# Mixer B's values through an SBUF copy, a gate tile between two head groups, and inverse square roots in eight operations

## The chip, the core and the metric

The kernel runs on one core of a Trainium2 chip. A core has five engines with queues of their own: PE (TensorE, matrix products; PEld is its loading of the stationary operand), ACT (ScalarE), DVE (VectorE), POOL (GpSimd) and SP (SyncE, which here issues most transfers). Products land in PSUM, eight banks of 128 x 512 float32; everything else works on SBUF. The metric is the device time of one execution in microseconds. Before the change it was 1541.07 us, the median of three runs (1538.99 to 1541.78).

## The reference

Two layers on an input of 512 tokens by 1024 channels. Each layer has a mixing half and a channel half, both with residual additions:

```python
h = rms_norm(x, norm_mix[l]);  z = h @ w_in[l]
qa, ka, va, qi, ki, wi, cq, ckv, kr, ga, gb = split_cols(z)
y_a = sparse_indexed_attention(...)          # mixer A: 8 heads, top 128 keys by an indexer
qb = (rms_norm(cq) @ b_w_uq[l])              # mixer B: 8 heads of 64 + 32 (rotated) columns
kv = (rms_norm(ckv) @ b_w_ukv[l])            # 64 key columns and 64 value columns per head
kb = concat(kv[..., :64], rope(kr));  vb = kv[..., 64:]
y_b = latent_attention(rms_norm(qb), rms_norm(kb), vb)
merged = sigmoid(ga + ...) * (y_a @ w_proj_a[l]) + sigmoid(gb + ...) * (y_b @ w_proj_b[l])
x = x + merged @ w_out[l]
u = causal_dwconv(rms_norm(x) @ w_up[l]);  x = x + (silu(u[..., d_ff:]) * u[..., :d_ff]) @ w_down[l]
```

The norm of a head's key takes the mean square over its 96 columns: 64 of its own and 32 rotated ones that all heads share. The norms' inverse square roots are what the change calls rsqrt.

## The kernel before, in words

**Products in two parts.** Float32 precision is had from PE's faster format by splitting every operand into a high part (a cast, ScalarE) and a low part (the operand minus its cast, VectorE) and adding three products: high by high, high by low, low by high. `split_into` (L299 to L306) is the helper for activations: the cast is L302, the subtraction L303; where a scale is applied they are L305 and L306. Weight tiles of up to 128 x 1024 are loaded by SP (L156) in the order of `dense_plan`, cast by ScalarE (L173), and their low part comes from VectorE (L185) or, for the kinds listed in `DL` (gb, ga, uv, ug, kv, uq), from a negated ScalarE copy (L201) onto which a DMA issued by POOL adds the tile (L202).

**PSUM.** Four rings of banks: D (2) for dense tiles, L (3) for scores and for mixer B's projections, T (2) for transposes and norm sums, Y (1) for attention outputs. A bank can be written again when every engine has read what was in it.

**Order.** The program is written as interleaved generators. `mix_dense` yields after every few matmuls; it produces the indexer's products, the latents, mixer B's two head groups (`attn_b(0)` and `attn_b(1)`), the eight gate tiles gb, mixer A's groups, and the gate tiles ga. While the attention heads of mixer B run (`mixer("yb", ...)`), a feeder calls `mix_dense` at a given rate per step, so that dense matmuls stand between those of the attention. `later(n, f)` puts a piece of work n steps further on. From this a scheduler makes the final order of every engine's queue; it may move an instruction ahead of others on its engine. The queues themselves run strictly in order. The indexer's top-k search (`top_k`, L1014 and L1021 on VectorE) is spread over the same steps.

**A head group of mixer B** (`attn_b`). For each of four blocks of 128 tokens, six matmuls (L834) write 256 key columns and 256 value columns of four heads into an L bank. Then:

```python
A.copy(k4[t][:, :, 0:64], p[:, 0:4])                            # L840
split_into(v[:, :, 0:64], v[:, :, 64:128], p[:, 4:8])           # L302 and, a step later, L303
squares(p[:, 0:4], ssk[:, t], 64)                               # L821, and L822 on VectorE
```

So two engines read the bank. The queries' four blocks follow: nine matmuls each (L871) into an L bank, a copy (L877) and squares (L821). `keys` (L848, L849) and `queries` (L896) make the mean squares, rsqrt gives the factors, and the keys (L858) and queries (L902) are scaled on VectorE; POOL rotates and completes them. `turn_b` transposes a head's queries and keys on PE (L1127) and splits them (tbh, tbl); `scores_b` computes scores in four blocks of 128 queries with 128, 256, 384 and 512 keys (L1142 to L1144, one L bank each), VectorE takes the maximum (L1145), and ScalarE the exponential with its sum (L357, an activation and a read of the accumulator). `softmax_end` normalises, `values` transposes the probabilities (L1052) and multiplies them with the values (L1059).

**rsqrt** (L331 to L346): a first guess by integer arithmetic (L334), then three Newton steps of three VectorE operations each (L343 to L345): ten operations on tiles of 128 x 4 or 128 x 16.

## Time and profile before

| what | value |
|---|---|
| median of the runs | 1541.07 us (1538.99 to 1541.78) |
| the profiled execution | 1542.47 us, of which the span is 1540.8 us |
| granted PE clock | 1.00 throughout |
| PE busy | 1528.9 us, 99% |
| VectorE / ScalarE / POOL busy | 1124.0 / 945.9 / 395.0 us |

The span goes from the first to the last instruction. In the rows below an instruction stands with its line, engine, operation, output and inputs; a wait row reads engine, tile and line, what it waited for, then microseconds in total, times, and the longest. PE's matmuls overlap, so a busy PE is not a PE at its peak, and a stop of PE is best measured from start to start.

### The profile page before, as it was taken

What the parts mean: (1) busy time and instruction counts of PE and PEld (TensorE: products, weight loads), DVE (VectorE), ACT (ScalarE), POOL (GpSimd) and SP (SyncE); (2) the same over time, 40 slices, a digit from 0 to 9 for tenths busy, and PEclk for the clock granted to TensorE, in tenths of its full rate; (3) what the DMA queues carried; (4) which work ended last, traced back from release to release, by engine and by line L of the source; (5) the groups of instructions that cost most, each with busy time, mean ns of one, the idle gap of its engine ahead of it and who ended that gap; (6) DMA issues with size and microseconds to landing.
All of it is one profiled execution on the core that took longest, in us unless ns stands there. A gap on an engine that the chain in (4) does not pass through costs nothing.

```text
span 1540.8 us, 23967 instructions
## 1 busy us (share of the span) xinstructions
PE 1528.9 (99%) x8666; PEld 1337.1 (87%) x8666; DVE 1124.0 (73%) x2303; ACT 945.9 (61%) x1553; POOL 395.0 (26%) x578
## 2 busy tenths in 40 slices
PE   9999999999999999999999999999999999999998
PEld 8887999888888898889998889998888888988898
DVE  7899988666476693547979999885574857845577
ACT  7756677773577536665557677686635765456642
POOL 2343012300012331125502520223001115311355
PEclk9999999999999999999999999999999999999999
DMA  7464124733478448873554641356435783588723
GB/s 245 104 160 122 46 92 110 186 120 119 127 189 190 103 117 219 191 178 96 151 165 112 166 99 56 103 135 173 131 99 144 177 190 95 152 197 195 176 77 109
DMA packets 73575, 216.29 MB, mean 140 GB/s; under 512 B 8432, under 2 KB 11504, under 8 KB 73456
## 3 DMA queue, kind: packets, MB, share of 16 engines
q1 hardware_dynamic: 54592, 149.08, 31.0%
q0 software_dynamic: 18432, 65.28, 22.6%
q8 instruction: 68, 1.11, 0.3%
q14 instruction: 51, 0.42, 0.1%
q10 hardware_dynamic: 432, 0.40, 0.1%
HBM read 141.06 MB, written 4.19 MB: 94 GB/s over the span
## 4 chain that ended last, share of the span: by engine, by line
PE 82%; DVE 12%; ACT 3%; issue 1%; POOL 0%; DMA 0%; DVEq 0%; ACTq 0%
PE D L516 35%; PE T L516 15%; PE D L539 6%; PE L L1424 5%; PE T L1424 4%; PE D L1424 3%; DVE sc L1021 2%; PE Y L1059 2%; DVE m L1014 2%; PE Y L1424 2%; PE T L1052 2%; PE L L516 2%; PE L L324 1%; PE L L323 1%; PE L L706 1%
## 5 line engine op out<-in xcount | busy, mean ns | idle before, releaser
L173 ACT CAST wh<-wr 128x1024 fp32r<-128x1024 f32 (+2 forms) x205 | 211.2, 1033 | 164.4 <-PE D L516 73.5
L202 POOL DMA_DIRECT2D wl<-wr x128 | 110.8, 877 | 633.0 <-ACT wl L201 604.4
L516 PE MATMUL D<-hxh,wh 128*128 128x512 f32 (+1 forms) x440 | 174.2, 396 | 0.0
L516 PE MATMUL D<-hxl,wh 128*128 128x512 f32 (+1 forms) x440 | 172.9, 393 | 0.0
L201 ACT ACTIVATE wl<-wr 128x1024 fp32r<-128x1024 f32 (+2 forms) x128 | 132.2, 1035 | 47.9 <-PE D L516 25.7
L191 ACT CAST wh<-wr 128x896 fp32r<-128x896 f32 x88 | 82.7, 941 | 103.8 <-POOL wr L215 69.6
L1093 POOL TENSOR_TENSOR P<-M,sel 128x128 f32<-128x128 f32 (+1 forms) x64 | 54.5, 907 | 272.9 <-DMA M<-in_bias_dram 239.3
L516 PE MATMUL D<-hxh,wl 128*128 128x512 f32 (+1 forms) x440 | 117.9, 393 | 0.0
L539 PE MATMUL D<-wh,hxh 128*128 128x256 f32 x384 | 113.8, 297 | 0.0
L196 DVE TENSOR_TENSOR wl<-wr,wh 128x896 fp32r<-128x896 f32 x88 | 103.8, 1181 | 8.2 <-ACT wh L191 3.1
L215 POOL TENSOR_TENSOR wr<-wr 128x256 f32<-128x256 f32 x88 | 93.8, 1068 | 60.8 <-DVE wr L214 48.3
L539 PE MATMUL D<-wl,hxh 128*128 128x256 f32 x384 | 109.3, 285 | 0.0
L539 PE MATMUL D<-wh,hxl 128*128 128x256 f32 x384 | 108.4, 283 | 0.0
L185 DVE TENSOR_TENSOR wl<-wr,wh 128x1024 fp32r<-128x1024 f32 x77 | 95.4, 1245 | 6.6 <-ACT wh L173 5.6
L516 PE MATMUL D<-hrl,wh 128*128 128x512 f32 x256 | 99.6, 389 | 0.0
L516 PE MATMUL D<-hrh,wh 128*128 128x512 f32 x256 | 99.6, 389 | 0.0
L516 PE MATMUL T<-hrh,wh 128*128 128x512 f32 x256 | 99.6, 389 | 0.0
L516 PE MATMUL T<-hrl,wh 128*128 128x512 f32 x256 | 99.6, 389 | 0.0
L516 PEld LDWEIGHTS D<-hxh,wh 128*128 128x128 f32 x440 | 82.9, 188 | 13.4 <-DVE gb L680 0.2
L516 PEld LDWEIGHTS D<-hxl,wh 128*128 128x128 f32 x440 | 82.9, 188 | 12.7
L516 PEld LDWEIGHTS D<-hxh,wl 128*128 128x128 f32 x440 | 80.2, 188 | 14.0
L1368 DVE SCALAR_TENSOR_TENSOR c<-T,vec,c 128x511 f32<-128x511 f32 x32 | 23.9, 748 | 89.1 <-ACT c L1365 89.1
(454 smaller groups left out, 4577.2 us busy)
## 6 DMA issues: line engine op xcount, KB each, us to landing
wr<-in_wd_dram SPq DMA_DIRECT2D x197, 512.0 KB, 3.7
wl<-wr POOLq DMA_DIRECT2D x120, 512.0 KB, 5.3
wr<-in_wd_dram SPq DMA_DIRECT2D x88, 256.0 KB, 2.6
x<-in_xT_dram SPq DMA_DIRECT2D x16, 256.0 KB, 4.8
M<-in_bias_dram SPq DMA_DIRECT2D x16, 256.0 KB, 4.0
wr<-in_wd_dram SPq DMA_DIRECT2D x7, 384.0 KB, 3.3
kah<-kah SPq DMA_DIRECT2D x16, 128.0 KB, 4.5
kal<-kal SPq DMA_DIRECT2D x16, 128.0 KB, 3.7
```

Source lines behind the costliest of these rows:

```text
L173: ins = self.nc.scalar.copy(h[:, :n], t[:, :n])
L185: eng.tensor_tensor(out=o[:, c], in0=t[:, c], in1=h[:, c].bitcast(F32), op=OP.subtract)
L191: self.nc.scalar.copy(h[:, :896], t[:, 128:1024])
L196: self.later(lag, lambda: self.nc.vector.tensor_tensor(out=o[:, :896], in0=t[:, 128:1024], in1=h[:, :896].bitcast(F32), op=OP.subtract))
L201: self.nc.scalar.activation(o, t, AF.Copy, scale=-1.0)
L202: self.nc.gpsimd.dma_start(o.bitcast(F32), t, accum_op=OP.add)
L215: g(2)(out=b[:, 6:8], in0=b[:, 0:3:2], in1=b[:, 3:6:2], op=OP.add)
L516: mm(p[:, t0:], lhsT=w, rhs=x[:, t0:], start=n == 0, stop=n == len(seq) - 1, skip_group_check=True)
L539: mm(pp[b][:, t, :], lhsT=x, rhs=w, start=n == 0 and half == 0 and t == 0, stop=n == 11 and half == 1, skip_group_check=True)
L1014: ins = V.max(out=m8[i], in_=st["sc"][i][:, :128 * (i + 1)])
L1093: G.tensor_tensor(out=P[:, P0[i]:P0[i] + w], in0=M[:, 512 - w:512], in1=sel[:, SEL0[i]:SEL0[i] + w], op=OP.add)
L1424: mm(p, lhsT=w, rhs=x, start=b0, stop=b1, skip_group_check=True)
```

## The change

Three edits, and one that follows from the third.

1. The value columns are copied out of PSUM by ScalarE into one half of an SBUF tile vr, which two token blocks share; the cast and the subtraction of the split read this copy.
2. GB_1 goes from 4 to 5: in the weight plan and in the program, the fifth gate tile (gb, 4) comes after `attn_b(0)` and before `attn_b(1)`, where before all of tiles 4 to 7 came after both.
3. rsqrt makes one Newton step and one step of third order: eight VectorE operations. It can write its result to a given tile, so the norm's copy into rstd (L467) goes.
4. The keys' mean square is one VectorE operation in place of two. The shared rotated part is divided by 96 and given its epsilon once per layer on POOL.

```diff
-NEWT = 1
+CUBE = 0.375 ** 0.5
-GB_1 = 4
+GB_1 = 5
-    def rsqrt(a, shape, quick=False):
+    def rsqrt(a, shape, out=None):
 
         y, t = small("y", shape), small("t", shape)
         V.tensor_scalar(y.bitcast(I32), a.bitcast(I32), -0.5, float(0x5F3759DF), op0=OP.mult, op1=OP.add)
...
-        for _ in range(3):
-            V.tensor_tensor(out=t, in0=y, in1=y, op=OP.mult)
-            V.scalar_tensor_tensor(t, t, -0.5, a, op0=OP.mult, op1=OP.mult)
-            V.scalar_tensor_tensor(y, t, 1.5, y, op0=OP.add, op1=OP.mult)
-        return y
+        V.tensor_tensor(out=t, in0=y, in1=y, op=OP.mult)
+        V.scalar_tensor_tensor(t, t, -0.5, a, op0=OP.mult, op1=OP.mult)
+        V.scalar_tensor_tensor(y, t, 1.5, y, op0=OP.add, op1=OP.mult)
+        V.tensor_tensor(out=t, in0=y, in1=y, op=OP.mult)
+        V.scalar_tensor_tensor(t, t, -CUBE, a, op0=OP.mult, op1=OP.mult)
+        V.scalar_tensor_tensor(t, t, 1.25 / CUBE, t, op0=OP.add, op1=OP.mult)
+        V.scalar_tensor_tensor(y if out is None else out, t, 1.875, y, op0=OP.add, op1=OP.mult)
+        return y if out is None else out
...
-            r = rsqrt(v, [4], quick=True)
-            V.tensor_copy(self.rstd, r)
+            rsqrt(v, [4], self.rstd)
...
-            later(6, lambda: V.tensor_reduce(out=ss, in_=t3, axis=AX.X, op=OP.add))
+
+            def key_sums():
+                V.tensor_reduce(out=ss, in_=t3, axis=AX.X, op=OP.add)
+                G.tensor_scalar(ss, ss, 1.0 / 96, EPS, op0=OP.mult, op1=OP.add)
+            later(6, key_sums)
...
-                split_into(v[:, :, 0:64], v[:, :, 64:128], p[:, 4:8])
+                if t % 2 == 0:
+                    vr = slot("vr")
+                raw = vr[:, t % 2 * 256:t % 2 * 256 + 256].rearrange("p (h c) -> p h c", c=64)
+                A.copy(raw, p[:, 4:8])
+                split_into(v[:, :, 0:64], v[:, :, 64:128], raw)
...
-                V.tensor_tensor(out=m, in0=ssk, in1=st["sskr"][:, :, None].to_broadcast([128, 4, 4]), op=OP.add)
-                V.tensor_scalar(m, m, 1.0 / 96, EPS, op0=OP.mult, op1=OP.add)
+                V.scalar_tensor_tensor(m, ssk, 1.0 / 96, st["sskr"][:, :, None].to_broadcast([128, 4, 4]),
+                                       op0=OP.mult, op1=OP.add)
```

Lines of the changed kernel lie up to five above and up to three below those of the kernel before: its values' matmuls are L833, its queries' L874, its dense matmuls L511, its scores L1145 to L1147.

The change moves instructions. On ScalarE, at the first two value blocks of group 1 in layer 0 (kn is the keys' copy, vr the new copy, vb the cast, sqb the squares, tbh a head's transposed queries), this stood before:

```order
L840 COPY kn_1258<-L_1272 128x4x64
L302 CAST vb_1266<-L_1272 128x4x64
L821 ACTIVATE sqb_1283<-L_1272 128x256
L840 COPY kn_1259<-L_1286 128x4x64
L302 CAST vb_1267<-L_1286 128x4x64
L821 ACTIVATE sqb_1310<-L_1286 128x256
```

and now:

```order
L839 COPY kn_1306<-L_1320 128x4x64
L844 COPY vr_1329<-L_1320 128x256
L302 CAST vb_1314<-vr_1329 128x4x64
L820 ACTIVATE sqb_1332<-L_1320 128x256
L302 CAST tbh_1369<-T_1364 100x512
L839 COPY kn_1307<-L_1335 128x4x64
L844 COPY vr_1329<-L_1335 128x256
L302 CAST vb_1315<-vr_1329 128x4x64
```

The cast of vb no longer reads the L bank, and there is one instruction more per block. A cast of head 0's transposed queries now stands between the two blocks.

On PE, behind the last queries' block of group 0 in layer 0 (L_1220 before, L_1219 now), before:

```order
L871 MATMUL L_1220<-wl_1002,cqh_869 128x384
L834 MATMUL L_1272<-wh_1043,ckvh_788 128x512
L834 MATMUL L_1272<-wh_1043,ckvl_789 128x512
L834 MATMUL L_1272<-wl_1044,ckvh_788 128x512
L834 MATMUL L_1272<-wh_1043,ckvh_792 128x512
```

and now:

```order
L874 MATMUL L_1219<-wl_998,cqh_865 128x384
L511 MATMUL D_1257<-hxl_147,wh_1039 128x512
L511 MATMUL D_1257<-hxh_162,wh_1039 128x512
L511 MATMUL D_1257<-hxl_163,wh_1039 128x512
L511 MATMUL D_1257<-hxh_170,wh_1039 128x512
```

Group 1's first value block began at once; now 23 of the gate tile's 24 matmuls come first.

On PE in head 0 of mixer B, at its first score blocks (L_1465 and L_1502 before; L_1461 is the third block now), before:

```order
L1144 MATMUL L_1465<-tbh_1457,tbl_1435 128x128
L871 MATMUL L_1471<-wh_1232,cql_870 128x384
L871 MATMUL L_1471<-wl_1121,cqh_684 128x384
L871 MATMUL L_1471<-wl_1121,cqh_778 128x384
L871 MATMUL L_1471<-wl_1233,cqh_869 128x384
L1142 MATMUL L_1502<-tbh_1457,tbh_1434 128x256
```

and now:

```order
L833 MATMUL L_1432<-wh_1121,ckvl_789 128x512
L833 MATMUL L_1432<-wl_1122,ckvh_788 128x512
L1145 MATMUL L_1461<-tbh_1387,tbh_1369 128x384
L1146 MATMUL L_1461<-tbl_1388,tbh_1369 128x384
L1147 MATMUL L_1461<-tbh_1387,tbl_1370 128x384
L874 MATMUL L_1468<-wh_1231,cqh_680 128x384
```

Before, group 1's value blocks were done by the first scores and only its last two queries' blocks stood among them. Now its last two value blocks and all four queries' blocks do.

More of the change, by code (lines that the diff above doesn't have):

```diff
@@ L329, in mm3 @@
         mm(p, lhsT=al, rhs=bh, start=False, stop=stop, skip_group_check=True)
-    def rsqrt(a, shape, quick=False):
+    def rsqrt(a, shape, out=None):
         y, t = small("y", shape), small("t", shape)
         V.tensor_scalar(y.bitcast(I32), a.bitcast(I32), -0.5, float(0x5F3759DF), op0=OP.mult, op1=OP.add)
-        if not (quick or NEWT):
-            for _ in range(3):
-                G.tensor_tensor(out=t, in0=y, in1=y, op=OP.mult)
-                G.tensor_tensor(out=t, in0=t, in1=a, op=OP.mult)
-                G.tensor_scalar(t, t, -0.5, 1.5, op0=OP.mult, op1=OP.add)
-                G.tensor_tensor(out=y, in0=y, in1=t, op=OP.mult)
-            return y
-        for _ in range(3):
-            V.tensor_tensor(out=t, in0=y, in1=y, op=OP.mult)
-            V.scalar_tensor_tensor(t, t, -0.5, a, op0=OP.mult, op1=OP.mult)
-            V.scalar_tensor_tensor(y, t, 1.5, y, op0=OP.add, op1=OP.mult)
-        return y
+        V.tensor_tensor(out=t, in0=y, in1=y, op=OP.mult)
[6 more added lines that the diff above has]
+        return y if out is None else out
     def pin(ins, i, k):
```

## The prediction

> **What bounds the kernel now.** I read the page first, then the waits of PE, then PE's timeline in the stage that the change touches, then ScalarE's and VectorE's timelines there.
>
> ```profile
> span 1540.8 us, 23967 instructions
> PE 1528.9 (99%) x8666; PEld 1337.1 (87%) x8666; DVE 1124.0 (73%) x2303; ACT 945.9 (61%) x1553; POOL 395.0 (26%) x578
> PE 82%; DVE 12%; ACT 3%; issue 1%; POOL 0%; DMA 0%; DVEq 0%; ACTq 0%
> ```
>
> PE is busy for 1528.9 of 1540.8 us, so the idle time that any reordering could remove is 11.9 us over the whole span. The chain of waits gives 12% to DVE (VectorE), but that does not mean that 12% can be had there: a chain that is followed back from one short stop of PE runs along the engine that caused the stop for as long as this engine was never idle. What a change in one stage is worth is the sum of PE's stops in it. The waits of PE name them:
>
> ```profile
> PE L L834 <- DVE vb L303: 1.2, 3, 0.6
> PE L L871 <- DVE vb L303: 0.5, 1, 0.5
> PE L L1142 <- ACT P L357: 0.6, 1, 0.6
> PE T L1127 <- DVE qn L902: 0.3, 2, 0.2
> PE L L1143 <- DVE tbl L306: 0.3, 1, 0.3
> ```
>
> Four stops, 1.7 us, are PE waiting for an L bank whose last reader is the VectorE subtraction that makes the low half of mixer B's values (vb). This is the longest of them in PE's timeline (start, duration, and idle time before it in brackets):
>
> ```profile
> 109.07 0.40 PE L516 MATMUL D<-hxl,wh 128*128 128x512 f32 x1
> 110.04 0.50 PE L834 MATMUL L<-wh,ckvh 128*128 128x512 f32 x1 [0.58 <-DVE vb L303]
> ```
>
> A stop costs more than the idle time shown, because a matmul's record reaches over the start of the next. Matmuls of 512 columns follow each other every 0.23 us (six of them take from 104.53 to 105.92, below), so the one at 110.04 was due at 109.07 + 0.23 = 109.30 and came 0.74 late, 0.16 more than the bracket says. I use idle time plus 0.16 per stop.
>
> **Term 1: the value copies.** Now ScalarE copies p[:,4:8] into an SBUF tile, and the cast (L302) and the VectorE subtraction (L303) read that tile. The L bank is then held by ScalarE alone, until its squares (L821) are done. Two rows show what this is worth at the stop of 110.04, which needed the bank of the first of these tiles:
>
> ```profile
> 107.39 0.39 ACT L840 COPY kn<-L 128x256 f32<-128x256 f32 x1
> 107.64 0.41 ACT L302 CAST vb<-L 128x256 fp32r<-128x256 f32 x1
> 107.91 0.43 ACT L821 ACTIVATE sqb<-L 128x256 f32<-128x256 f32 x1
> ...
> 109.58 0.41 DVE L303 TENSOR_TENSOR vb<-L,vb 128x256 fp32r<-128x256 f32 x1
> ```
>
> ScalarE had read the tile by 107.91 + 0.43 = 108.34, before PE wanted it at 109.30; VectorE held it until 109.99. With the extra copy (0.26 from start to start, like the steps from 107.39 to 107.91) ScalarE is done at 108.60, still in time. So all four stops go: 1.7 + 4 x 0.16 = **-2.3 us**.
>
> What it adds is 16 copies on ScalarE. The nearest rows:
>
> ```profile
> L840 ACT COPY kn<-L 128x256 f32<-128x256 f32 x16 | 6.0, 375 | 2.5 <-PE L L834 2.3
> L302 ACT CAST vb<-L 128x256 fp32r<-128x256 f32 x16 | 6.2, 390 | 0.0
> L302 ACT CAST b11h<-c 128x256 fp32r<-128x256 f32 x22 | 8.8, 399 | 0.1
> L303 DVE TENSOR_TENSOR vb<-L,vb 128x256 fp32r<-128x256 f32 x16 | 6.5, 409 | 0.0
> L303 DVE TENSOR_TENSOR b11l<-c,b11h 128x256 fp32r<-128x256 f32 x22 | 9.2, 420 | 3.3 <-ACT b11h L302 3.3
> ```
>
> The copy has the shape of L840: 16 x 0.375 = 6.0 us of ScalarE's busy time, or 2.1 us per layer counted from start to start (8 x 0.26). The b11 rows are the same cast and subtraction from SBUF in the channel mixer: 399 against 390 and 420 against 409 ns. So I take the source as worth nothing on either engine (+0.3 us in all if the 9 and 11 ns are real). [...]
>
> **Term 2: shorter inverse square roots.** Ten VectorE operations become eight, the copy into rstd goes, and the keys' two preparing operations become one (the constant part moves to POOL, one small operation per layer). L343 stands 66 times, three to a call, so there are 22 calls: 44 + 4 + 4 = 52 VectorE operations fewer.
>
> ```profile
> L343 DVE TENSOR_TENSOR t<-y x66: 143/164/464, 32.5 to 1189.8; 128x16 f32<-128x16 f32 x48, 128x4 f32<-128x4 f32 x18
> ```
>
> At the median of 164 ns that is some 8.5 us of VectorE. Outside mixer B they are worth nothing: PE has other matmuls and no stop names a norm; without that cover the two ends of a layer would gain at most the two operations and the copy, 0.5 us each. Inside, the two calls of a head group put at least 5 x 0.16 = 0.8 us less in front of the scaled queries (qn) and the transposed keys (tbl), for which PE stops 0.3 + 2 x 0.16 and 0.3 + 0.16. VectorE is the full engine there:
>
> ```profile
> 104.00:112.00 8.00, 7.42 (x33) 5.72 (x33) 8.00 (x32) 6.54 (x17) 6.88 (x19) 1.00 0.79 172
> 112.00:120.00 8.00, 7.85 (x42) 6.29 (x41) 8.00 (x30) 4.43 (x11) 5.42 (x15) 1.00 0.72 187
> ```
>
> (length, then busy time of PE, PEld, DVE, ACT, POOL: 8.00 of 8 us for DVE in both.) The lateness is up to 0.6 per stop and the relief 0.8, and the gate's tile puts PE work before them. I take all of it: **-1.1 us**; the other bound is 0, if the list of VectorE's work is merely filled with top-k operations instead.
>
> **Term 3: the gate's tile between the groups.** With GB_1 = 5 a gate tile of 24 matmuls (5.4 us, on D banks) stands between group 0 and group 1 of mixer B's projections. Its weight load (SP) and the DMA that makes its low half (POOL) move one tile ahead on their queues:
>
> ```profile
> wl<-wr POOLq DMA_DIRECT2D x120, 512.0 KB, 5.3
> ```
>
> Such a DMA lands 5.3 us after its issue, and PE reads the low half only in the last eight of a gate tile's matmuls. No PE wait of the list names a DMA, so I cost both at nothing; a tile that came too late would cost up to those 5.3 us. The same matmuls run in all. But group 1's eight tiles, which use the three L banks, start 5.4 us later and now stand among the score tiles of heads 0 and 1, which use the same banks; the gate matmuls that stood there have gone ahead. The bank of every tile there is freed by ScalarE, in its queue's order. Its steps, from start to start, and PE's:
>
> ```profile
> 126.67 2.00 ACT L201 ACTIVATE wl<-wr 128x1024 fp32r<-128x1024 f32 x2
> 128.56 0.47 ACT L877 COPY qn<-L 128x384 f32<-128x384 f32 x1
> 128.92 0.51 ACT L821 ACTIVATE sqb<-L 128x384 f32<-128x384 f32 x1
> 129.31 0.60 ACT L357 ACTIVATE P<-L,mx 128x384 f32<-128x384 f32 x1
> 129.77 0.23 ACT L357 ACTIVATION_READ_ACCUMULATOR P<-L,mx 128x1 f32 x1
> 129.86 0.71 ACT L357 ACTIVATE P<-L,mx 128x512 f32<-128x512 f32 x1
> ```
>
> ```profile
> 102.97 0.33 PE L871 MATMUL L<-wh,cqh 128*128 128x384 f32 x1
> ...
> 104.53 0.39 PE L834 MATMUL L<-wh,ckvh 128*128 128x512 f32 x1
> ...
> 105.92 0.39 PE L834 MATMUL L<-wh,ckvh 128*128 128x512 f32 x1
> ```
>
> So a weight cast of 1024 columns takes ScalarE 0.95, an exponential of 384 columns with its sum 0.55 (0.36, 0.45 and 0.66 for 128, 256 and 512, by 0.1 per 128 columns), a queries' tile 0.36 + 0.38; a queries' tile takes PE 1.56 and a values' tile 1.39. I follow the new order in layer 0 from the end of group 1's third values' tile (0). ScalarE: keys, values, exponential of scores 0, cast, squares, to 1.4; exponential of scores 1, a cast of transposed keys, two weight casts, to 4.3; then keys and values of the fourth tile, exponential of scores 2, cast and squares, ending at 6.1. PE: scores 1, seven transposes, the fourth tile (0.1 late), scores 2, a queries' tile, five transposes and two gate matmuls, to 5.3; then scores 3 need the fourth tile's bank: a stop of 0.8. In head 1, scores 1 wait in the same way for the exponential of scores 0, behind two queries' copies and the normalising of head 0's last block: 11.0 against 10.35, 0.65. Together 1.5 in layer 0, and by the same walk 1.5 in layer 1, where the load of the exponential's table (1.28) falls into the same queue: **+3.0 us**, with 0 as the lower bound if the order places each tile just where its bank is free. Stops of the same kind go, because these heads are laid out anew:
>
> ```profile
> 126.34 0.49 PE L1127 MATMUL T<-ident,qn 128*100 128x128 f32 x3
> 126.83 0.50 PE L1142 MATMUL L<-tbh,tbh 100*128 100x512 f32 x1
> ...
> 134.12 0.50 PE L1142 MATMUL L<-tbh,tbh 100*128 100x512 f32 x1 [0.57 <-ACT P L357]
> ```
>
> 0.32 at 126.83 (three transposes take 0.17) and 0.57 + 0.16 at 134.12: **-1.05**.
>
> **The sum** is -2.3 - 1.1 + 3.0 - 1.05 = -1.4 us. The profiled execution took 1542.5 us, 1.4 over the median of 1541.07; the same difference from the median gives **1539.7 us**.
>
> **The rivals.** (a) *The old stops go and no new ones come*: term 3's lower bound, -2.3 - 1.1 - 1.05 = -4.4, so 1536.6 us. For it: ScalarE is idle for 1.5 to 3.6 us in each of the two windows above, and the order interleaves by readiness. Against: ScalarE is fuller in the next window, where group 1's tiles now go (6.59 of 8 us, next fence). (b) *Swap without gain*: VectorE's lateness stays and ScalarE's stops come in full: -2.3 + 3.0 - 1.05 = -0.3, so 1540.7 us. (c) *Slower*: ScalarE becomes the bound of heads 0 and 1.
>
> ```profile
> 120.00:128.00 8.00, 7.74 (x47) 6.53 (x46) 7.75 (x24) 6.59 (x14) 6.32 (x17) 1.00 0.17 63
> ```
>
> In the new order ScalarE has, from the same zero to the last scores of head 1, 34 instructions of 16.6 us by the steps above, PE 13.5. If PE waits out the whole excess, 3.1 per layer, the time is 1541.07 + 6.2 - 2.3 = 1545.0 us. It decides from the point where more than about one tile in three waits for its bank; against it, the end of that list is a cast of probabilities, a cast of weights and an exponential that none of these tiles waits for. (d) *The copy does not free the bank*, since squares come last on ScalarE: the four stops stay, 1541.9 us; the rows at 108.34 and 109.99 speak against it.
>
> **How the numbers follow.** Chances: the forecast 0.42, (a) 0.29, (b) 0.17, (c) 0.09, (d) 0.03. 0.2% is 3.1 us, about what a measurement of this kernel can tell from no change. Forecast, (b) and (d) lie within it, (a) beyond it, (c) beyond it on the other side; some of (a) may fall short, as some of the forecast may fall over: faster 0.29, same 0.61, slower 0.10. The range leaves out (c) and the far ends: from 1536.0 (a, 0.6 lower for the runs' spread) to 1543.0 (forecast, with term 2 at zero and half a microsecond more per layer of ScalarE's stops, and the spread of the runs).
>
> **What would show it.** Right: no PE wait on vb; VectorE 52 and ScalarE 16 instructions apart from before; PE waits for L banks naming ScalarE (P, sqb) at scores 3 of head 0 and scores 1 of head 1, of 0.5 to 0.8 us; PE's timeline the same outside the stretches around 91 to 160 and 859 to 925 us. Wrong: PE waits of over 3 us per layer there (c), none at all (a), or a difference that arises in mixer A or the channel mixer, whose instruction order is nearly untouched.

## The result and the profile after

The changed kernel takes 1550.66 us, the median of six executions, one of which, at 1943.3 us and a mean granted clock of 0.72, is not in the ratio (the other five have a median of 1550.18). Beside it the kernel before took 1540.07 us. The ratio is 1.0067, 95% interval 1.0056 to 1.0078: slower by 10 us, where 1.4 us of gain were forecast.

The page of the profile after, in the lines that answer to those shown of before (span, busy time, chain of waits):

```profile
span 1549.7 us, 23926 instructions
PE 1531.6 (99%) x8666; PEld 1341.1 (87%) x8666; DVE 1121.3 (72%) x2251; ACT 952.0 (61%) x1569; POOL 394.8 (25%) x580
PE 83%; DVE 12%; ACT 2%; DMA 1%; issue 1%; POOL 0%; DVEq 0%; ACTq 0%; SPq 0%
```

The counts are those of the edits: 52 VectorE instructions fewer, 16 ScalarE instructions and two of POOL more, the same matmuls. The shares hardly differ, so the page alone does not tell where 9 us of span went. The waits of PE in the changed kernel do; these are the ones that are new or differ (engine, tile, line, what for: total, times, longest):

```profile
PE T L1130 <- DVE qn L905: 8.2, 2, 4.1
PE Y L1062 <- DVE ptl L303: 1.5, 2, 1.1
PE T L770 <- DVE ptl L303: 0.7, 2, 0.3
PE D L1500 <- DVE wl L196: 0.6, 1, 0.6
PE L L874 <- ACT P L353: 0.4, 1, 0.4
PE L L1145 <- ACT P L353: 0.3, 1, 0.3
```

No stop for vb is left. In its place stand two stops of 4.1 us, one in each layer, where PE begins to transpose head 0's queries and VectorE has not scaled them yet. PE's timeline there in layer 0, of the changed kernel and then of the kernel before:

```profile
112.82 0.39 PE L511 MATMUL D<-hxl,wh 128*128 128x512 f32 x1
117.34 0.45 PE L1130 MATMUL T<-ident,qn 128*100 128x128 f32 x1 [4.13 <-DVE qn L905]
```

```profile
116.08 0.39 PE L516 MATMUL D<-hxh,wh 128*128 128x512 f32 x1
116.32 0.31 PE L1127 MATMUL T<-ident,qn 128*100 128x128 f32 x1
```

PE is there 3.3 us earlier than before (last matmul at 112.82 against 116.08), and gets its queries 1 us later. Some 1.0 of the 3.3 us is less work: by the columns of its matmuls up to here, PE has four and a half of 512 columns fewer ahead of the transposes (0.23 us each). The rest is the stops for vb that are gone. VectorE's timeline in the same place of the changed kernel, from the last of the four sums of squares of the queries to their scaling:

```profile
109.08 0.53 DVE L821 TENSOR_REDUCE ssq<-sqb 128x4 f32<-128x384 f32 x1
...
113.03 0.67 DVE L1024 MATCH_REPLACE8 sc<-m,sc 128x512 f32<-128x512 f32 x1
...
113.71 0.68 DVE L679 TENSOR_TENSOR gb<-D,row 128x512 f32<-128x512 f32 x1
...
114.46 0.53 DVE L1024 MATCH_REPLACE8 sc<-m,sc 128x384 f32<-128x384 f32 x1
...
115.48 0.68 DVE L1017 MAX8 m<-sc 128x8 f32<-128x512 f32 x1
116.09 0.40 DVE L303 TENSOR_TENSOR vb<-vr,vb 128x256 fp32r<-128x256 f32 x1
116.41 0.40 DVE L821 TENSOR_REDUCE ssk<-sqb 128x4 f32<-128x256 f32 x1
116.74 1.01 DVE L905 TENSOR_TENSOR qn<-qn,y 128x384 f32<-128x384 f32 x2
```

VectorE is not idle for a moment in this stretch. Top-k steps, the evacuation of the gate's tile that now stands here, and the first block of group 1 are in its queue ahead of the queries' scaling: 7.66 us from the sum at 109.08 to the scaling at 116.74. In the kernel before it was 6.62:

```profile
109.11 0.54 DVE L822 TENSOR_REDUCE ssq<-sqb 128x4 f32<-128x384 f32 x1
...
115.73 0.54 DVE L902 TENSOR_TENSOR qn<-qn,y 128x384 f32<-128x384 f32 x1
```

What fills the two stretches differs (summed from start to start). Before, four blocks of group 1 stood in it (vb and ssk, eight operations, 2.6 us), and three top-k operations (1.0 us). Now one block of group 1 is left (0.65 us), and in the place of the others stand eight top-k operations (2.5 us) and the gate's evacuation (0.6 us). The four scalings of the keys take 1.9 us where they took 1.3, and the inverse square root with its mean square 1.5 us in nine operations where it took 1.2 in eleven: single operations are longer here, beside a POOL that works without a gap (7.97 us of the 8 from 104 to 112, 6.88 before).

In layer 1 the same stretch takes 8.98 us (7.04 before), and the list of operations does not explain it. One scaling of the keys takes 3.14 us:

```profile
878.88 3.14 DVE L861 TENSOR_TENSOR kn<-kn,y 128x256 f32<-128x256 f32 x1
```

Its neighbours take 0.41 to 0.45. That is 2.7 us longer, in a stop of 4.1; the last section comes back to it.

The stops cost more than their 8.2 us. The profile by stretches of 2 us (length, then busy time and instructions of PE, PEld, DVE, ACT, POOL; granted PE clock; DMA share; GB/s), layer 0 and then layer 1 of the changed kernel:

```profile
114.00:116.00 2.00, 0.00 (x0) 0.00 (x0) 2.00 (x9) 0.00 (x0) 0.00 (x0) 1.00 1.01 277
116.00:118.00 2.00, 0.66 (x3) 0.66 (x4) 2.00 (x6) 0.00 (x0) 0.00 (x0) 0.50 0.69 143
118.00:120.00 2.00, 2.00 (x9) 1.62 (x8) 2.00 (x6) 0.00 (x0) 0.00 (x0) 0.50 0.07 14
120.00:122.00 2.00, 2.00 (x6) 1.53 (x5) 0.92 (x4) 1.36 (x4) 0.00 (x0) 0.50 0.52 178
122.00:124.00 2.00, 2.00 (x10) 1.60 (x9) 2.00 (x6) 1.71 (x4) 0.20 (x1) 0.79 0.22 88
...
886.00:888.00 2.00, 0.67 (x4) 0.61 (x5) 2.00 (x7) 0.00 (x0) 0.00 (x0) 0.85 1.00 262
888.00:890.00 2.00, 2.00 (x9) 1.58 (x8) 1.67 (x5) 0.00 (x0) 0.00 (x0) 0.50 0.75 172
890.00:892.00 2.00, 2.00 (x9) 1.53 (x9) 1.25 (x4) 1.84 (x6) 0.00 (x0) 0.79 0.27 31
```

The granted clock falls to half, in layer 0 during the stop (at 116.0 us), in layer 1 as it ends (at 887.4), and stays there for 5.5 us of PE's work in layer 0 (from 117.34 to 122.8) and 3.4 us in layer 1 (to 890.8). Matmuls of 512 columns follow each other every 0.43 us there (four steps from 120.79 to 122.50), where 0.23 is usual. So half of that time, 4.5 us in all, is by estimate the most that the slow clock can have cost by itself; some of it was time in which PE waited for the next scaled queries anyway.

A table of progress shows where the kernels part. It is worked out from PE's rows of each trace: the time at which PE had issued a given amount of matmul work (by columns), minus the time at which the first profile of before had. The rows are named by that profile's time. The other kernels are told of below (the redrawn ones have the same work in another order); "before, again" is a second profile of the same kernel, and shows how far two executions differ.

| at (us in before) | before, again | changed | value copies only | all, top-k held (e11) | changed, redrawn (e17) | all, top-k held, redrawn (e19) | before, queries one tick earlier (e16) |
|---|---|---|---|---|---|---|---|
| 86.5 | -0.9 | +0.3 | 0.0 | +0.3 | +0.4 | -0.3 | -0.3 |
| 108.3 | -0.9 | -1.2 | -1.4 | -1.2 | -1.1 | -1.7 | -0.3 |
| 133.1 | -0.6 | +3.4 | +2.2 | 0.0 | +3.6 | -0.3 | -0.5 |
| 180.4 | -0.7 | +5.2 | +1.4 | -0.1 | +3.8 | -1.4 | -0.5 |
| 869.0 | -1.3 | +5.1 | +1.0 | +0.1 | +4.2 | -1.3 | +1.8 |
| 892.6 | -1.3 | +9.5 | +3.4 | +1.3 | +5.3 | -0.3 | +1.8 |
| 963.6 | -1.3 | +10.1 | +3.9 | +3.9 | +6.4 | +0.3 | +2.4 |
| 1032.3 | -0.2 | +11.3 | +5.9 | +5.4 | +8.4 | +2.9 | +3.9 |
| 1525.8 | -1.4 | +10.0 | +4.7 | +4.3 | +7.2 | +1.6 | +3.6 |
| end | -3.1 | +9.1 | +2.9 | +2.6 | +5.7 | -0.1 | +1.9 |

The changed kernel is 1.5 us ahead of its own start at 108 us (+0.3 to -1.2): the stops for vb are gone and their time is won. Between 108 and 133 us it loses 4.6, between 869 and 893 us 4.4: the two stops with what follows them. Some 2 us more go between 133 and 180 us. The 1.2 us between 964 and 1032 us are not the change's: the second profile of the kernel before has the same swing there (-1.3, -0.2, and -1.4 again at 1526).

### The profile page after: what moved, and what is told of

Its sections match the earlier page's. It is cut to its first block, busy times and chain, and to the rows that moved or that the text cites. A ratio compares the mean times of both kernels' runs of the same rounds, so it can differ in the third digit from the quotient of the medians.

```text
span 1549.7 us, 23926 instructions
## 1 busy us (share of the span) xinstructions
PE 1531.6 (99%) x8666; PEld 1341.1 (87%) x8666; DVE 1121.3 (72%) x2251; ACT 952.0 (61%) x1569; POOL 394.8 (25%) x580
## 4 chain that ended last, share of the span: by engine, by line
PE 83%; DVE 12%; ACT 2%; DMA 1%; issue 1%; POOL 0%; DVEq 0%; ACTq 0%; SPq 0%
PE D L511 37%; PE T L511 15%; PE D L534 7%; PE L L1427 4%; PE T L1427 3%; PE Y L1062 3%; DVE sc L1024 2%; PE D L1427 2%; PE T L1055 2%; DVE m L1017 2%; PE L L511 2%; PE Y L1427 1%; DMA wr<-in_wd_dram 1%; PE L L323 1%; PE L L324 1%
## 5 line engine op out<-in xcount | busy, mean ns | idle before, releaser
L173 ACT CAST wh<-wr 128x1024 fp32r<-128x1024 f32 (+1 forms) x205 | 211.6, 1035 | 162.5 <-PE D L511 76.2
L511 PE MATMUL D<-hxh,wh 128*128 128x512 f32 (+1 forms) x440 | 175.6, 399 | 0.0
L511 PE MATMUL D<-hxl,wh 128*128 128x512 f32 (+1 forms) x440 | 174.4, 396 | 0.0
L511 PE MATMUL D<-hxh,wl 128*128 128x512 f32 (+1 forms) x440 | 118.1, 393 | 0.0
L511 PE MATMUL D<-hrl,wh 128*128 128x512 f32 x256 | 99.6, 389 | 0.0
L511 PE MATMUL D<-hrh,wh 128*128 128x512 f32 x256 | 99.6, 389 | 0.0
L511 PE MATMUL T<-hrh,wh 128*128 128x512 f32 x256 | 99.6, 389 | 0.0
L511 PE MATMUL T<-hrl,wh 128*128 128x512 f32 x256 | 99.6, 389 | 0.0
L511 PEld LDWEIGHTS D<-hxl,wh 128*128 128x128 f32 x440 | 84.0, 191 | 13.7 <-issue 0.6
L511 PEld LDWEIGHTS D<-hxh,wh 128*128 128x128 f32 x440 | 83.8, 191 | 13.6 <-issue 0.2
L511 PEld LDWEIGHTS D<-hxh,wl 128*128 128x128 f32 x440 | 80.0, 188 | 13.7
```

The source lines that it names most:

```text
L173: ins = self.nc.scalar.copy(h[:, :n], t[:, :n])
L511: mm(p[:, t0:], lhsT=w, rhs=x[:, t0:], start=n == 0, stop=n == len(seq) - 1, skip_group_check=True)
```

## The experiments

All numbers in one table; the kernel before stood beside every run, at 1539.5 to 1540.8 us. "Queries" are PE's waits T <- DVE qn: total, and the longest.

| kernel | median us | ratio to before, 95% | queries, us |
|---|---|---|---|
| changed | 1550.7 | 1.0067 (1.0056 to 1.0078) | 8.2, 4.1 |
| e1_gb4: without the gate's tile | 1548.3 | 1.0055 (1.0040 to 1.0070) | 7.6, 4.6 |
| e2_gate_only | 1547.1 | 1.0046 (1.0029 to 1.0062) | 5.2, 2.8 |
| e3_copy_only | 1545.6 | 1.0040 (1.0025 to 1.0055) | 6.1, 3.3 |
| e4_rsqrt_only | 1543.4 | 1.0025 (1.0016 to 1.0034) | 0.3, 0.3 |
| e5_gap18: changed, 18 steps ahead | 1550.5 | 1.0069 (1.0053 to 1.0086) | 5.6, 2.7 |
| e6_hold: changed, top-k held at rounds 11, 9 | 1549.4 | 1.0062 (1.0047 to 1.0077) | 3.3, 1.6 |
| e11_hold_l1: changed, held at 11, 10 | 1546.1 | 1.0032 (1.0021 to 1.0044) | 3.2, 1.4 |
| e7_hold_gb4: e1, held at 11, 9 | 1546.4 | 1.0044 (1.0029 to 1.0059) | 2.6, 1.3 |
| e10_hold_gb4_l1: e1, held at 11, 10 | 1544.5 | 1.0024 (1.0015 to 1.0034) | 2.6, 1.3 |
| e8_hold_before: before, held at 11, 9 | 1542.9 | 1.0026 (1.0016 to 1.0035) | 0.6, 0.2 |
| e9_keep25: changed, matmuls in the stop | 1560.0 | 1.0122 (1.0107 to 1.0137) | 1.2, 0.5 |
| e12_before_again | 1539.7 | 1.0000 (0.9990 to 1.0010) | 0.4, 0.2 |
| e14_before_gap13: before, redrawn | 1541.8 | 1.0007 (0.9998 to 1.0017) | too short to be listed |
| e16_before_lag21: before, redrawn | 1545.5 | 1.0032 (1.0022 to 1.0041) | too short to be listed |
| e17_after_gap13: changed, redrawn | 1546.6 | 1.0038 (1.0025 to 1.0051) | 6.7, 4.1 |
| e18_hold_gap13: e10, redrawn | 1543.8 | 1.0025 (1.0015 to 1.0034) | 2.4, 1.3 |
| e19_all_hold_gap13: e11, redrawn | 1542.7 | 1.0015 (1.0006 to 1.0025) | 2.4, 1.3 |
| e20_copy_gap13: e3, redrawn | 1549.5 | 1.0059 (1.0042 to 1.0076) | 11.9, 6.7 |

### Each part alone

The first theory (A) was that the gate's tile is to blame. Four kernels take the change apart. The first puts the gate's tile back and keeps the rest; the others put one part into the kernel before.

```diff
 e1_gb4, to the changed kernel
-GB_1 = 5
+GB_1 = 4
 e2_gate_only, to the kernel before
-GB_1 = 4
+GB_1 = 5
 e3_copy_only, to the kernel before
-                split_into(v[:, :, 0:64], v[:, :, 64:128], p[:, 4:8])
+                if t % 2 == 0:
+                    vr = slot("vr")
+                raw = vr[:, t % 2 * 256:t % 2 * 256 + 256].rearrange("p (h c) -> p h c", c=64)
+                A.copy(raw, p[:, 4:8])
+                split_into(v[:, :, 0:64], v[:, :, 64:128], raw)
 e4_rsqrt_only: the hunks of the change in rsqrt, its callers and keys(), to the kernel before
```

> The change without its middle part: the value copies and the shorter inverse square root stay, the gate's tile stands behind both groups again. Theory A (the gate's tile brings TensorE to head 0's query transposes before VectorE has scaled the queries, two stops of about 4.1 us): the two stops of T <- DVE qn go back to below 1 us each and the time to 1537 to 1541 us, against 1550.7 with the whole change. Theory B (the added ScalarE copies delay what TensorE waits for): still about 1548 to 1551. Theory C (the shorter inverse square root and the reordered key sums put other work ahead of the queries' scaling on VectorE): still about 1548 to 1551.

> The kernel before with the gate's tile alone moved between the two groups. Theory A: two stops of T <- DVE qn of 3 to 5 us, one in each layer, time 1546 to 1552. Theories B and C: no such stops, time 1539 to 1542; the waits for vb stay as before.

> The kernel before with the value copies alone. Theory A: the four stops for vb go, 1537 to 1540 us (term 1 of the prediction: -2.3). Theory B: 1548 to 1551. Theory C: as A.

> The kernel before with the shorter inverse square root and the moved key sums alone. Theory A: 1538.5 to 1541 (term 2 of the prediction: -1.1, which may be less because its gain was tied to the gate's tile). Theory C: 1548 to 1551, with stops at T <- DVE qn. Theory B: as A.

All four are slower than before, and no theory has all four as they came. The three single parts lose 7.6, 6.2 and 3.9 us, 17.7 together, far more than the whole change. Theory A falls: without the gate's tile the two stops are still there (7.6 us), and the value copies alone bring them too. One wait row each, of the value copies alone and of the gate's tile alone:

```profile
PE T L1131 <- DVE qn L906: 6.1, 2, 3.3
```

```profile
PE T L1127 <- DVE qn L902: 5.2, 2, 2.8
```

Theory B (the copies delay ScalarE) and theory C (the rsqrt edits reorder VectorE) fit no better: three unlike kernels have the same stop for VectorE, and the fourth, the shorter inverse square roots alone, costs 4 us without it. There the stops for vb, which the subtraction on VectorE ends, grow from 1.7 to 3.0 us in all. The column "value copies only" of the table shows the pattern: 1.4 us ahead at 108 us, 2.2 behind at 133. The waits for vb had let PE arrive at the transposes when VectorE was ready. Without them PE arrives earlier (its last matmul ahead of the transposes starts at 113.14 instead of 116.08, of which 0.7 us is three matmuls fewer), and VectorE, which was busy all along, is no earlier: its scaling starts at 115.75 in this kernel and at 115.73 in the kernel before. In the kernel without the gate's tile, the stop of 4.6 us in layer 0 comes behind a scaling of the keys that took 2.63 us, like the one of 3.14 above.

### Taking work off VectorE's queue

Theory D: VectorE is full in the 22 us ahead of the queries' scaling, and its place in that queue sets the time. The test leaves all work in, but issues the later top-k rounds behind the scaling of group 0's queries:

```diff
+HOLD = [10, 8]
...
                     for t in range(4):
-                        (G if "Q" in POOL else V).tensor_tensor(out=q4[t][:, :, 0:96], in0=q4[t][:, :, 0:96],
+                        last = V.tensor_tensor(out=q4[t][:, :, 0:96], in0=q4[t][:, :, 0:96],
                                         in1=r[:, t, :, None].to_broadcast([128, 4, 96]), op=OP.mult)
+                    st["scaled", g] = last.ins
...
-        for _ in range(TOPK // 8):
+        for n in range(TOPK // 8):
+            while n == HOLD[l] and ("scaled", 0) not in st:
+                yield
             for i in (3, 2, 1):
-                with low():
+                with tc.issue_after(st["scaled", 0]) if n == HOLD[l] else low():
                     ins = V.max(out=m8[i], in_=st["sc"][i][:, :128 * (i + 1)])
```

HOLD counts from zero: 10 and 8 are the 11th round of layer 0 and the 9th of layer 1. The rival (E) gives PE more work ahead of the transposes instead (GAP_B = 12 becomes 18).

> The changed kernel with one constraint on VectorE's order: from the 11th round in layer 0 and the 9th in layer 1, the top-k rounds are issued behind the scaling of group 0's queries (13 and 14 top-k operations fewer ahead of it, some 6.5 us of VectorE). All of the change stays in. Theory D (after the four first runs: VectorE has no idle time in the 22 us before the queries' scaling, top-k operations stand ahead of it in its queue, and every stop of TensorE that is removed earlier comes back at head 0's query transposes): the two stops of T <- DVE qn fall from 4.1 us to below 0.5 each, the time falls by 6 to 9 us to 1542 to 1545 us. Theory E (TensorE's own order is at fault, too little work in front of the transposes, and VectorE would be late anyway): the stops stay above 3 us, 1548 to 1551.

> The changed kernel with 18 in place of 12 steps of the gate's and group 1's matmuls issued ahead of head 0's query transposes; VectorE's top-k work is as before. Theory D: the stop at the first transposes shrinks, but VectorE stays full and the stops return later in heads 0 and 1 (for tbl, P or vb): 1546 to 1550 us. Theory E: the two stops vanish and nothing comes in their place: 1542 to 1544 us.

> As the run with the held top-k rounds, but with the gate's tile back behind both groups: value copies, shorter inverse square roots and held top-k. Theory D: no stop for vb and none above 0.5 us for qn, 1536 to 1540 us, below the kernel before. Theory E: about 1548, as without the hold.

> The kernel before with the held top-k rounds alone. Theory D: the four stops for vb stay or shrink, those for qn go: 1538 to 1540 us, a gain of 0 to 2 us, because TensorE reached the query transposes only when VectorE was ready. Theory E: 1539 to 1541, no change.

More work ahead of the transposes helps nothing: 1550.5, far above theory E's range and half a us above D's. The stops for the queries shrink from 8.2 to 5.6 us, and others come, though not at the tiles that D named. The hold shortens the stops to 1.6 us at most, where less than 0.5 was expected, and both held kernels miss D's range: the time falls by 1.3 us with the gate's tile and by 1.9 without. The progress of PE splits this: without the gate's tile, the held kernel is 1.0 us ahead of before at 180 us (2.2 behind without the hold), still 0.8 ahead at 869, and then loses 7.1 up to 1032 us. In layer 1 the hold was too long: the held rounds end late, beside mixer B's last heads. The last top-k operation of layer 1, in the changed kernel and in the one with the hold:

```profile
940.18 0.41 DVE L1024 MATCH_REPLACE8 sc<-m,sc 128x256 f32<-128x256 f32 x1
```

```profile
983.55 0.41 DVE L1028 MATCH_REPLACE8 sc<-m,sc 128x256 f32<-128x256 f32 x1
```

The next two kernels shorten the hold in layer 1 by one round (HOLD = [10, 9]), without the gate's tile and with it.

> Value copies and shorter inverse square roots, the gate's tile behind both groups, top-k held behind the queries' scaling from round 11 in layer 0 and, unlike the earlier run with 9, from round 10 in layer 1. In layer 0 the earlier run stood 1.0 us ahead of the kernel before at the same matmul, and lost 6 us in layer 1, where the held rounds came back late. Theory D: layer 0 as there, layer 1 loses 1 to 3 us: 1541 to 1544 us. If the layer 1 loss does not come from the hold: 1546 to 1547 as before.

> The whole change, with the hold at rounds 11 and 10. Theory D: between the run without the gate's tile and 1549.4 (hold at 11 and 9): 1545 to 1548 us; what it stands above the run without the gate's tile, 1.5 to 4 us, is what the tile costs when the queries are not late. If the tile costs nothing then: within 1 us of that run.

They take 1544.5 (half a us above its range) and 1546.1 us (in its range). For the whole change the hold is worth 4.6 us, with an edit that moves nothing but top-k rounds in the program. The table of progress shows it at the two places: between 108 and 133 us the held kernel loses 1.2 us instead of 4.6, between 869 and 893 us 1.2 instead of 4.4. From 893 to 1032 us it loses 4.1, where the changed kernel loses 1.8. The scheduler's answer to the hold is more than the rounds, though: in layer 0 PE comes to the transposes with nine matmuls of 512 columns fewer behind it. And the first hold in the kernel before, which has no such stop, costs 3 us, where a gain of 0 to 2 was expected.

### The clock by itself

Theory F was that the fall of the clock behind the stop has a price of its own. The test fills the stop with matmuls whose results are overwritten:

```diff
+KEEP = 25
...
             p = bank("T")
+            for _ in range(KEEP if h == 0 and x is qn else 0):
+                tc.keep_in_program_order(mm(p, lhsT=nrm.h[0][:, 0:128], rhs=nrm.h[0], start=True, stop=True))
             for t in range(4):
```

> The changed kernel with 25 idle-time matmuls of 512 columns (5.7 us, their results are overwritten) in TensorE's queue ahead of head 0's query transposes of each layer, where it stops for 4.1 us now. Nothing is done earlier. Theory F (a stop of this length costs more than its own length, because the granted TensorE clock falls to 0.50 for some 5 us after it: 116 to 123 us and 887 to 891 us in the changed kernel's trace): the clock stays at 1.00 in both stretches, and the time falls by 3 to 5 us to 1546 to 1548. Theory G (the granted clock costs nothing of its own, because other engines pace these stretches): no change, 1550 to 1552, or more where the added matmuls end later than the queries are ready.

It missed, and tells nothing of the clock's price. PE did keep its pace through the filled stop (in layer 0 the 25 matmuls take 5.83 us, 0.23 from start to start), but it had less of its own work ahead of the transposes (in layer 0 nine matmuls of 512 columns) and between them and the next head's (five instead of eleven), so that it stopped at the next head's instead, for VectorE again:

```profile
PE T L1133 <- DVE tbl L304: 5.3, 2, 2.9
```

In layer 0 this stop is 2.42 us long (to 123.36), and behind it two matmuls of 512 columns start 0.57 us apart. The mean granted clock of the execution is 0.998, as against 1.000 in the kernel before.

What speaks on the price is the list of executions of one and the same kernel. Of 97 timed executions of the kernel before, 93 had a mean granted clock of 1.000 and a median of 1539.9 us (at most 1542.4); the other four had 0.999 and took 1543.2, 1543.4, 1544.0 and 1545.1. Of the four executions with the value copies alone, three had 0.999 (1544.4 to 1545.8 us) and one 0.995 (1548.5). With the same instructions in the same order, an execution with a lower mean clock was 3 to 5 us longer. That is no experiment (what made it fall may also have cost time), so the share of the clock in the 10 us stays open between 0 and the 4.5 worked out above.

### Redrawing the order

Why should the hold, or a shorter inverse square root, cost the kernel before 3 to 4 us without bringing the stop? Each of them makes the scheduler put out another order: by the traces, another matmul stands at 642 (hold) and 404 (inverse square root) of PE's 8666 places. So the next kernels change the order and nothing else, by one step more ahead of head 0 (1091 places) or by the queries' scaling given to the scheduler one tick earlier (364 places). Such a kernel is called redrawn here.

```diff
 e14_before_gap13, to the kernel before; e17_after_gap13, to the changed kernel
-GAP_B = 12
+GAP_B = 13
 e16_before_lag21, to the kernel before
-LAG_S = 22
+LAG_S = 21
 e12_before_again: nothing
```

> The kernel before, unchanged, for a second profile of it. All theories: 1539.5 to 1541 us, ratio 1.000. Its trace shows what of the first profile (1542.5 us) was that execution's own: probably the stop of 1.5 us for wl at the end.

> The kernel before with 13 in place of 12 steps of other matmuls ahead of head 0: 546 of TensorE's order rows differ, no work is added or removed. Theory H (any redrawn order costs about 3 us): 1541.5 to 1545 us. Theory I (the parts of the change cost what they cost by a mechanism of their own): 1539 to 1541.

> The kernel before with the scaling of the queries given to the scheduler one tick earlier: 104 of TensorE's order rows differ. Theory H: 1541 to 1545 us. Theory I: 1539 to 1541.

> The changed kernel with 13 in place of 12 steps ahead of head 0. Theory H: its order is an ordinary draw already, so a redraw moves it by 2 us at most either way, 1548.5 to 1552.5. The two stops of 4 us stay in all theories.

The redraws move the kernel before by +2.0 us (its interval touches no change) and +5.7, half a us above theory H's range, and the changed kernel by -4.1, more than theory H allowed. What the changed kernel wins by its redraw has a place and a row. Between 869 and 893 us it loses 1.1 instead of 4.4; VectorE has the same list of operations there between the last sum and the queries' scaling, but it takes 6.78 us in place of 8.98, the keys' scaling that took 3.14 us takes 0.41, and the stop is 2.5 us instead of 4.1:

```profile
878.66 0.41 DVE L861 TENSOR_TENSOR kn<-kn,y 128x256 f32<-128x256 f32 x1
```

The last column of the table of progress shows where the kernel before with the queries one tick earlier loses: not at the queries, but by small stops from 180 us on, in mixer A's first heads and again late in layer 1:

```profile
PE T L1052 <- DVE kal L782: 1.6, 2, 0.8
PE T L771 <- DVE ptl L303: 1.0, 2, 0.5
PE T L771 <- DVE kal L782: 0.9, 2, 0.5
```

All of them wait for VectorE. The kernel before in its old order has few of these. So a difference of 2 to 6 us between two kernels with unlike orders is by itself no proof of the mechanism that the edit had in mind. The second profile of the kernel before is 3.1 us shorter than the first, 0.9 of it in the first 24 us and 1.7 behind 1525 us, where the stop of 1.5 us for wl is gone: the profile on which the forecast rests was a long execution of that kernel.

The last three put the same redraw on partial versions.

```diff
 e18, to e10 (copies, rsqrt, held top-k); e19, to e11 (whole change, held top-k); e20, to e3 (copies only)
-GAP_B = 12
+GAP_B = 13
```

> Value copies, shorter inverse square roots and held top-k rounds (11 and 10), the gate's tile behind both groups, redrawn with 13 steps ahead of head 0. Theory H (any order is a draw of some us): 1539.5 to 1547 us, that is 1544.5 give or take 3. If it comes below 1539 it beats both kernels. If the order before were the best in reach: not below 1540.

> The whole change with held top-k rounds, redrawn in the same way (1546.1 with 12 steps). Theory H: 1543 to 1549; no stop for qn above 1.5 us and a clock of 1.00 at 110 to 125 us and 880 to 895 us.

> The kernel before with the value copies alone, redrawn in the same way (1545.6 with 12 steps). The stop for qn in layer 0 stays at 2 to 4 us under theory D, whatever the draw; time 1542 to 1548.

The whole change with the held rounds, redrawn, takes 1542.7 us, 7.9 below the changed kernel and still 2.7 above the kernel before. In its VectorE timeline the queries' scaling follows the last sum after 3.0 us instead of 7.7, and only the operations of the inverse square root and its mean square stand between them.

```profile
107.00 0.54 DVE L822 TENSOR_REDUCE ssq<-sqb 128x4 f32<-128x384 f32 x1
...
109.96 1.15 DVE L906 TENSOR_TENSOR qn<-qn,y 128x384 f32<-128x384 f32 x2
```

No stop for the queries is longer than 1.3 us, and the granted clock is 1.00 there:

```profile
110.00:112.00 2.00, 1.54 (x8) 1.00 (x6) 2.00 (x4) 1.97 (x6) 2.00 (x7) 1.00 1.02 192
112.00:114.00 2.00, 1.01 (x7) 0.82 (x8) 2.00 (x4) 1.04 (x4) 2.00 (x6) 1.00 0.76 117
114.00:116.00 2.00, 1.95 (x10) 1.40 (x8) 2.00 (x7) 1.36 (x4) 0.41 (x2) 1.00 0.98 305
```

With the long stops gone, the gate's tile moves the time in no steady direction: with it 1.6 us more at 12 steps (e11 against e10), 1.1 us less at 13 (e19 against e18, which took 1543.8, inside its range). No version came below the kernel before. Against the second profile of the kernel before, the held and redrawn kernel is level at 869 us (-1.3 in both), 1.0 us behind at 893 and 3.0 behind from 1032 us to the end. The cause of that was not settled.

The value copies alone went the other way, from 1545.6 to 1549.5, and outside what was expected: stops of 6.7 and 5.2 us. The last section says what its trace shows there.

## Why the prediction was wrong

The step that failed is one that no term has: the prediction took VectorE's scaled queries as ready when PE comes to head 0's query transposes. Before, PE waited there for 0.3 us in all, and term 2 let even that go. In the changed kernel it waits 8.2 us, 4.1 in each layer.

**Term 1, the value copies (-2.3).** The mechanism was right: no stop for vb is left, the copy frees the bank, and by 108 us the changed kernel had won 1.5 us. The prices were right: a copy took 381 ns (375 forecast), the subtraction 415 (409 before), the cast 410 (390 before). What failed is the sum behind it: a stop removed was booked as time won to the end. It is won only up to the next place where PE waits for the engine that is really behind. VectorE was full from 104 to 120 us, as the prediction's own rows showed, and the queries' scaling did not come earlier because PE did.

**Term 2, the shorter inverse square root (-1.1).** The prediction said of the scaled queries and transposed keys that "the gate's tile puts PE work before them. I take all of it". The 52 instructions are gone, but the time from the last sum to the scaled queries grew from 6.6 to 7.7 us in layer 0 and from 7.0 to 9.0 in layer 1. The other bound that the prediction named, a list "merely filled with top-k operations instead", is what happened in layer 0 (eight of them where three stood), and the gate's evacuation came in as well, while three of group 1's four blocks left. In layer 1 the one long scaling of the keys came on top. And PE had less before the transposes, not more: in layer 0 it arrived at 112.8 instead of 116.1.

**Term 3, the gate's tile (+3.0 - 1.05).** Stops that name ScalarE at L banks came, but 0.4 and 0.3 us in place of 3.0, and the old one of 0.57 went. The walk through ScalarE's and PE's queues took VectorE as ready everywhere. VectorE was the late engine.

**What a stop costs.** The prediction priced every stop at its idle time plus 0.16 us. That held for stops under 1 us (in the kernel before, the ones at 95.83 and 874.28, 0.20 and 0.41 by their brackets, came 0.37 and 0.57 late). At the stops of 4 us the granted clock fell to 0.50, which the prediction's price has no place for: up to 2.7 us more in layer 0 and 1.7 in layer 1.

**The sum and the rivals.** The forecast said -1.4, the runs say +10. Rival (c) had the right sign, from PE waits of over 3 us per layer, but less than half the size and the wrong engine: ScalarE in the forecast, VectorE in the trace. None of the rivals (a), (b) and (d) has a new stop for VectorE at the queries either. The places were right: nearly all is lost inside the two stretches that the prediction named (91 to 160 and 859 to 925 us). And it took the order as given: redraws of 2 to 6 us that no edit intends were in no term and not in the range.

How much of the 10 us is the late queries? The changed kernel loses 9.0 us in the two places. The kernel before, redrawn, loses 0.4 at most there, so another order alone does not bring this. With the rounds held the changed kernel loses 2.4: that makes 6.6 us of late queries with what follows them, the clock included. The time fell by less, 4.6 us, since the held kernel loses more from 893 us on. At 13 steps the redrawn changed kernel loses 5.8 in the two places and the held one 2.4, and the time fell by 3.9 us (1546.6 to 1542.7). So the late queries are the main part in both layers. Why VectorE is late is shown in layer 0, by what stands in its queue. In layer 1 the redraw without any hold, in which the long scaling of the keys is gone, loses only 1.1 us, so that there this one operation, more than the queue, made the difference; why it came up is open. What remains of the 10 us is of the size that the redraws have, and the runs do not tell it from them.

## What to carry to other kernels

A wait that ends early only helps if the next thing waited for is early too: ask of the engine that is busy without a gap what stands in its queue ahead of the next product that PE needs, in the new order, and count the backlog at the moment when PE arrives. Where a scheduler sets the order, time one or two redraws that do no other work before a gain or a loss of a few us is put down to an edit. Bulk work that is always ready (here the top-k rounds) should be held behind the product on the critical path; a hold that is a round too long can come back later (1549.4 against 1546.1 us here).

## What the runs showed of the hardware

**The clock fell at stops of PE of 2.4 to 6.7 us, and the length did not decide alone.** In layer 1 PE stopped for 3.0 us in the kernel without the gate's tile and kept its clock; with the gate's tile alone it stopped for 2.4 us (5.2 in all less the longest, 2.8) and lost it. Before the fall of the clock at 885.0 us PE was at work until 882.2 and again from 884.57. The first kernel's stretches, then the second's:

```profile
878.00:880.00 2.00, 1.59 (x9) 1.14 (x7) 2.00 (x8) 1.97 (x5) 2.00 (x8) 1.00 0.99 268
880.00:882.00 2.00, 0.00 (x0) 0.00 (x0) 2.00 (x8) 1.16 (x4) 1.63 (x5) 1.00 0.80 154
882.00:884.00 2.00, 1.40 (x8) 0.88 (x9) 2.00 (x5) 0.00 (x0) 2.00 (x5) 1.00 1.05 272
```

```profile
882.00:884.00 2.00, 0.15 (x1) 0.00 (x0) 2.00 (x10) 0.00 (x0) 0.00 (x0) 1.00 0.89 260
884.00:886.00 2.00, 1.43 (x8) 1.14 (x9) 2.00 (x7) 0.00 (x0) 0.00 (x0) 0.75 0.88 188
886.00:888.00 2.00, 2.00 (x7) 1.56 (x6) 1.51 (x5) 0.54 (x1) 0.00 (x0) 0.50 0.12 27
```

Five falls of the clock can be followed to their end, all to 0.50. By the trace's record of the clock they last 6.83 and 3.41 us in the changed kernel; by the clocks of the 2 us stretches it is 3.4 us in the kernel with the gate's tile alone, and 6.8 us in both layers of the redrawn kernel with the value copies alone, at its stops of 6.7 and 5.2 us. Why 2.4 us sufficed in one place and 3.0 did not in another was not shown.

**A small VectorE operation took 18 times its usual time beside GpSimd.** In the redrawn kernel with value copies alone, an operation of 128 x 16 in the queries' inverse square root took 2.92 us, where 0.16 is usual (18 times as long), while POOL ran its rotations without a gap:

```profile
114.85 2.92 DVE L343 TENSOR_TENSOR t<-y 128x16 f32<-128x16 f32 x1
```

```profile
114.53 0.71 POOL L890 TENSOR_TENSOR qn<-qn,rotn 128x64 f32<-128x64 f32 x1
...
117.30 0.39 POOL L893 TENSOR_TENSOR qn<-qn,rot 128x64 f32<-128x64 f32 x1
```

VectorE's operation ended at 117.77, as POOL's run did (its last product at 117.69). In layer 1 another took 2.11 us. This kernel's two stops (6.7 and 5.2) are 3.9 and 1.9 us longer than those of the same edit in its first order (2.9 and 3.3), and the two operations are 2.8 and 1.9 us longer than usual. The keys' scaling of 3.14 us in the changed kernel stands in such a place too: POOL runs its rotations from 878.31 to 882.25 us without a gap, and the operation (878.88) ends at 882.02.

```profile
878.31 0.98 POOL L887 TENSOR_TENSOR rot<-qn,rotn 128x64 f32<-128x64 f32 x1
...
880.93 1.32 POOL L857 TENSOR_TENSOR kn<-kr,y 128x128 f32<-128x128 f32 x2
```

What makes these operations long was not tested, and it does not strike each time: in the redrawn changed kernel the same scaling takes 0.41 us beside a run of POOL that has no gap either, and there it is POOL's products that are long (up to 1.90 us, where 0.32 is usual). An input in SBUF in place of PSUM did not show by itself: the subtraction of the value copies, which reads two SBUF tiles where it read one and a PSUM bank, took 415 ns in the changed kernel against 409 before.
